# Two blocks of layer 0's modulation: from TensorE in the attention to VectorE, ScalarE and an adding DMA in the projections

## The chip, the cores and the metric

The kernel runs on 1 core of one Trainium2 chip. The metric is device time in microseconds (us), taken as the median of several runs; the kernel before took 1288.5 us (3 runs, 1287.41 to 1289.77). The profile is one further execution, and its times count from the start of its span.

## The reference

One inference step of a small diffusion backbone with two layers, all in float32, on 512 latent tokens and 128 context tokens (640 in all, width 1024). Layer 0 is multi-head latent attention beside chunked spatial gating, layer 1 a pooling mixer; each is followed by a squared-ReLU MLP of width 4096. What matters here is the modulation, which every layer computes from the conditioning vectors and uses around both of its halves:

```python
mod = (jax.nn.silu(cond) @ w_mod[l] + b_mod[l]).reshape(-1, 1, N_MOD * D_MODEL)
sh1, sc1, g1, sh2, sc2, g2 = jnp.split(mod, N_MOD, axis=-1)
h = rms_norm(x, norm1_g[l]) * (1 + sc1) + sh1
x = x + g1 * mix                       # mix: attention and gating, or pooling
h = rms_norm(x, norm2_g[l]) * (1 + sc2) + sh2
x = x + g2 * squared_relu_mlp(h, w_ff1[l], w_ff2[l])
```

There are two conditioning vectors (one for latent, one for context tokens), so `mod` is two rows of 6 x 1024 numbers per layer. The six blocks are counted j = 0 to 5 below: j=2 is g1 and j=3 is sh2. Of layer 0, j=2 is first used in the residual add behind the output projection (`wo`), j=3 in the norm that follows it.

## The kernel before

**Order of the work.** TensorE runs the stages one after the other, and its products stand in the order in which the program writes them, as do the operations of every other engine: the schedule is written out by hand. After the loading and transposing of x and the first two blocks of the modulation (j = 0 and 1) come the products with `w_in`: `kv`, then `qa` (line 966 on), `v` and `u` (`z_block`, line 833), then `q` from `w_qx`, the gating, keys and values, the attention in 40 steps (line 1377 on), the output projection with `w_out`, and the two MLPs. A float32 product is made as three passes over a high and a low part of each operand (`mm3`, lines 828 to 830).

**Weights.** The class `Weights` (line 137) holds one list of items, in the order in which they are to be handled. An item's 512 KB or less are loaded by SP into a raw buffer (line 190); then the item is handled by `pump` (line 196): for a weight, ScalarE rounds it to a high part (line 218) and VectorE subtracts (line 228) into a slot of the weight pool. An item with a `use` of its own, as a block of the modulation, needs no slot. There are 5 raw buffers (`RAWB`); `raw_cap` bounds how many are out at a time, and an item can bring its own cap (`caps`), which then stays. `loads` issues the next loads in list order whenever `used` gives a buffer back in the program's order; on the chip SP's queue waits there until the buffer's last reader is done. `pump(n)` handles up to n items and stops at a full pool or at the held item; `need` handles items until the wanted one is there. Where an item's `use` returns a second half (`rest`), `pump` handles the following item between its two halves, and then skips its next call. In the projections the pool has 4 slots, and `pump(2)` stands behind each of the four qa, v and u items (each item is two k of 128 rows).

**The modulation of layer 0, j = 2 to 5.** `add_mod` puts 16 items into the list, eight for g=1 (j = 2, 3) and eight for g=2 (j = 4, 5). Each loads two raw buffers of 512 KB, and `mod_use` (line 361) multiplies them on TensorE: four products of 32 x 512 columns, one in each quarter of the array (line 367). After the eighth, the sum is copied, transposed by `mod_end` (line 387) and the bias added. The items are held (`st.hold`) until the projections are done and run in the attention's steps, one in each step but two of six.

**The modulation of layer 1.** `vmods` makes it without TensorE. Block j has eight items (k = 0 to 7) of one raw buffer each, and `vmod_use` (line 473) does for each: VectorE multiplies by the first conditioning vector's weight and adds to `acc[0]` (line 482; at k=0 it only multiplies, line 480); ScalarE multiplies the buffer in place by the second one (line 487; at k=0 into `acc[1]`); GpSimd adds it to `acc[1]` (line 489). Both sums lie in raw buffers. `st.later` counts handled items: three after the last block `vmod_sum` adds up the 128 rows on TensorE (line 499), four after it `vmod_end` transposes and adds the bias. These 48 items stand between the weights of layer 0's MLP, from block 1 on, one behind each weight, with a cap of 3 raw buffers. In that MLP `pump` stands behind each pair of products, and each tile of weights serves both parts of the 640 tokens.

**An adding DMA** is used in one place before (line 225): where `lo` is None, at the start of layer 1's MLP, GpSimd's queue adds `w_ff` from memory to the negated high part.

The lines that the change and the steps of the prediction touch are: 196 to 250 (`pump`), 473 to 526 (`vmod_use`, `vmod_sum`, `vmod_end`, `vmods`), 536 to 560 (the list), 833 (`z_block`), 920 (`kv_post`, whose last scaling is line 941), 950 (`ckv_post`: transposes on TensorE, evacuated by lines 956 and 957, run from the steps of `bg` within qa), 966 to 984 (qa), 996 (`qa_post`), 1034 (v's gelu), 1038 (`v_post`).

## Time and profile before

| | us |
|---|---|
| median of 3 runs | 1288.5 (1287.41 to 1289.77) |
| the profiled execution | 1284.05 |
| its span, first to last instruction | 1281.8 |
| TensorE busy in the span | 1253.5 |
| VectorE busy | 815.1 |
| ScalarE busy | 555.1 |
| GpSimd busy | 199.7 |

The rows further down come from a page of the profile and from more detailed answers on the same trace. PE is TensorE's matmul side, PEld its weight loads, DVE VectorE, ACT ScalarE, POOL GpSimd, SP the queue that issues most loads. `L367` is line 367 of the kernel; `out<-in` names tiles, `x128` counts instructions. A row of a timeline begins with the start and the duration in us. In rows of one line or tile the three numbers with slashes are the shortest, median and longest duration in ns, followed by the starts of the first and the last in us. A float32 product by `mod_use` or `vmod_sum` is recorded as two instructions, so four products count x8. Products overlap in TensorE's pipeline, so the busy time of a group is less than count times duration. "DMA to landing" counts from the issue of a DMA to its completion; the shares of DMA queues are shares of the 16 engines' time in the stretch. The granted clock is given as a share of 2.4 GHz.

### The profile page before, as it was taken

To read this page: it belongs to the slowest core of one execution; us is meant where nothing else is said; L and a number is where in the kernel's file an instruction comes from. 1 tells how busy PE (TensorE), PEld (TensorE's weight loads), DVE (VectorE), ACT (ScalarE), POOL (GpSimd) and SP (SyncE) were. 2 spreads that over 40 slices of the span, in tenths; PEclk is the share of its full clock that TensorE was granted. 3 is DMA by queue.
4 is the path that set the end of the run, shared out by engine and by line. 5 is a ranking of instruction groups with operands and counts; after the bars stand their busy time and mean duration, and the time that the engine had idled before them with its cause. 6 is when DMAs were issued, how large, how long until landed. Compare 5 with 4: busy or idle time off the path is not lost.

```text
span 1281.8 us, 20770 instructions
## 1 busy us (share of the span) xinstructions
PE 1253.5 (98%) x8308; PEld 1181.9 (92%) x8308; DVE 815.1 (64%) x1557; ACT 555.1 (43%) x1001; POOL 199.7 (16%) x178
## 2 busy tenths in 40 slices
PE   6999999999999999999999999999999999999997
PEld 5899875689999999999999999879999999999997
DVE  5753864564776565656565637676887666676664
ACT  4445454553453434334343423834235425254253
POOL 0010322221113131313231324310000000000001
PEclk9999999999999999999999999799999999999998
DMA  8742297350335444444444440912213232132212
GB/s 303 261 162 68 81 233 253 123 186 13 118 117 153 127 132 133 147 133 148 132 148 126 154 148 5 235 25 66 66 34 99 64 101 68 64 100 70 95 33 83
DMA packets 65375, 154.08 MB, mean 120 GB/s; under 512 B 5200, under 2 KB 22096, under 8 KB 64768
## 3 DMA queue, kind: packets, MB, share of 16 engines
q1 hardware_dynamic: 61360, 142.53, 34.0%
q0 software_dynamic: 3632, 10.16, 3.8%
q8 instruction: 65, 1.06, 0.3%
q14 instruction: 30, 0.25, 0.1%
q10 hardware_dynamic: 288, 0.08, 0.0%
HBM read 144.21 MB, written 5.39 MB: 117 GB/s over the span
## 4 chain that ended last, share of the span: by engine, by line
PE 84%; DVE 8%; ACT 5%; issue 1%; DMA 1%; POOL 0%; DVEq 0%; ACTq 0%; POOLq 0%
PE dn_ps L829 12%; PE dn_ps L828 12%; PE dn_ps L830 12%; PE up_ps L828 8%; PE up_ps L830 8%; PE up_ps L829 8%; PE o_ps L1329 1%; PE wo_ps L828 1%; PE wo_ps L829 1%; PE wo_ps L830 1%; PE mod_ps L367 1%; PE t_ps L1296 1%; DVE w L586 1%; PE s_ps L828 1%; PE v_ps L828 1%
## 5 line engine op out<-in xcount | busy, mean ns | idle before, releaser
L828 PE MATMUL dn_ps<-aa,w 128*128 128x320 f32 (+4 forms) x1024 | 318.3, 311 | 0.0
L829 PE MATMUL dn_ps<-aa,w 128*128 128x320 f32 (+4 forms) x1024 | 317.7, 310 | 0.0
L830 PE MATMUL dn_ps<-aa,w 128*128 128x320 f32 (+4 forms) x1024 | 317.0, 310 | 0.5 <-DVE w L228 0.5
L828 PE MATMUL up_ps<-h,w 128*128 128x320 f32 (+2 forms) x800 | 249.9, 312 | 1.3 <-ACT h L775 1.3
L829 PE MATMUL up_ps<-h,w 128*128 128x320 f32 (+2 forms) x800 | 248.0, 310 | 1.1 <-DVE h L779 1.1
L830 PE MATMUL up_ps<-h,w 128*128 128x320 f32 (+2 forms) x800 | 248.7, 311 | 0.2 <-DMA w<-w_ff 0.2
L1434 DVE SCALAR_TENSOR_TENSOR x<-dn_ps,mod,x 128x328 f32<-128x328 f32 (+5 forms) x360 | 145.4, 435 | 117.6 <-PE dn_ps L830 116.7
L828 PEld LDWEIGHTS dn_ps<-aa,w 128*128 128x128 f32 x1024 | 193.1, 189 | 1.8 <-issue 0.8
L830 PEld LDWEIGHTS dn_ps<-aa,w 128*128 128x128 f32 x1024 | 193.0, 188 | 0.8 <-DVE w L228 0.8
L829 PEld LDWEIGHTS dn_ps<-aa,w 128*128 128x128 f32 x1024 | 193.0, 188 | 0.1
L228 DVE TENSOR_TENSOR w<-raw,w 128x1024 fp32r<-128x1024 f32 (+4 forms) x122 | 151.9, 1249 | 46.4 <-ACT w L218 45.3
L218 ACT ACTIVATE w<-raw 128x1024 fp32r<-128x1024 f32 (+4 forms) x131 | 132.7, 1026 | 109.7 <-DMA raw<-w_ff 84.9
L828 PEld LDWEIGHTS up_ps<-h,w 128*128 128x128 f32 x800 | 151.2, 189 | 4.9 <-issue 3.4
L829 PEld LDWEIGHTS up_ps<-h,w 128*128 128x128 f32 x800 | 151.4, 189 | 1.6 <-DVE h L779 1.6
L830 PEld LDWEIGHTS up_ps<-h,w 128*128 128x128 f32 x800 | 151.0, 189 | 0.5 <-DMA w<-w_ff 0.5
L489 POOL TENSOR_TENSOR acc<-acc,raw 128x1024 f32<-128x1024 f32 x42 | 100.7, 2398 | 303.6 <-ACT raw L487 299.9
L581 ACT ACTIVATE w<-raw 128x512 fp32r<-128x512 f32 x84 | 51.0, 625 | 108.5 <-DVE raw L588 108.5
L487 ACT ACTIVATE raw<-raw,cs 128x1024 f32<-128x1024 f32 x42 | 48.3, 1149 | 63.3 <-DVE acc L482 58.8
L1963 POOL TENSOR_TENSOR y<-y,fg 128x1024 f32<-128x1024 f32 x1 | 2.4, 2395 | 406.9 <-ACT y L1959 406.9
L1508 DVE TENSOR_TENSOR r<-r,up_ps 128x328 f32<-128x328 f32 (+2 forms) x80 | 37.4, 484 | 40.2 <-ACT r L1507 38.4
L1511 DVE TENSOR_TENSOR aa<-r,aa 128x640 fp32r<-128x640 f32 (+3 forms) x52 | 39.7, 764 | 35.6 <-ACT aa L1510 35.6
L586 DVE TENSOR_TENSOR w<-raw,w 128x512 fp32r<-128x512 f32 x84 | 57.7, 687 | 6.8 <-ACT w L581 5.1
(404 smaller groups left out, 2100.3 us busy)
## 6 DMA issues: line engine op xcount, KB each, us to landing
raw<-w_ff SPq DMA_DIRECT2D x126, 512.0 KB, 3.8
raw<-w_mod SPq DMA_DIRECT2D x80, 512.0 KB, 3.8
raw<-w_m SPq DMA_DIRECT2D x16, 512.0 KB, 6.4
raw<-w_out SPq DMA_DIRECT2D x8, 512.0 KB, 4.6
w<-w_ff POOLq DMA_DIRECT2D x8, 512.0 KB, 9.8
kT<-ckvT POOLq DMA_DIRECT2D x4, 768.0 KB, 10.9
xr<-x SPq DMA_DIRECT2D x5, 512.0 KB, 5.4
xs<-x SPq DMA_DIRECT2D x2, 1280.0 KB, 8.9
```

The costliest lines, as they stand in the source:

```text
L218: self.nc.scalar.activation(out=hi, in_=r, func=AF.Copy)
L228: lambda: eng.tensor_tensor(out=lo, in0=r, in1=hi.bitcast(F32), op=ALU.subtract)
L487: act(out=raw if k else acc[1], in_=raw, func=AF.Copy, scale=w[1])
L489: nc.gpsimd.tensor_tensor(out=acc[1], in0=acc[1], in1=raw, op=ALU.add)
L581: act(out=w[:, 0], in_=src, func=AF.Copy)
L586: vec.tensor_tensor(out=w[:, 1], in0=src, in1=w[:, 0].bitcast(F32), op=ALU.subtract)
L828: mm(ps, lhsT=st_[0], rhs=mv[0], start=first, stop=False, skip_group_check=on)
L829: mm(ps, lhsT=st_[0], rhs=mv[1], start=False, stop=False, skip_group_check=on)
L830: mm(ps, lhsT=st_[1], rhs=mv[0], start=False, stop=last, skip_group_check=on)
L1434: vec.scalar_tensor_tensor(out=xv, in0=ps[:, p0:p0 + c1 - c0], scalar=gate[:, d, m:m + 1], in1=xv, op0=ALU.mult, op1=ALU.add)
L1508: vec.tensor_tensor(out=rv, in0=rv, in1=ps, op=ALU.mult)
L1511: vec.tensor_tensor(out=aa[:, 1, lo:hi], in0=r[:, lo:hi], in1=aa[:, 0, lo:hi].bitcast(F32), op=ALU.subtract)
```

## The change

The list of items is changed: the eight g=1 items leave it, and 16 items of the kind of layer 1 (j=2 and j=3 of layer 0, eight blocks each) are put between the weights of the projections by `add_vm`, two behind each of the qa items, of v's last and of u's first three. They bring the cap of 3. In the list, with V for a block: kv7, qa0, V, V, qa2, V, V, qa4, V, V, qa6, V, V, v0, v2, v4, v6, V, V, u0, V, V, u2, V, V, u4, V, V, u6, wq0 and so on. `pump(4)` stands where `pump(2)` stood behind qa, v and u items; the `pump(2)` behind kv stays. Between the halves of a block `pump` handles the following item only if that is a weight. For layer 0 and layer 1 alike, GpSimd's addition becomes a DMA of its queue that adds the raw buffer to `acc[1]`. The junk output of `v_post`'s squares goes into vn, as the scratch row is now used by `vmod_sum` in that stage.

```diff
@@ -63,6 +63,7 @@
 SPLIT = 3
 SLOW = "ws", "wkv"
 VM_AT = 11, 64
+VM_Z = {("qa", 0): 2, ("qa", 2): 2, ("qa", 4): 2, ("qa", 6): 2, ("v", 6): 2, ("u", 0): 2, ("u", 2): 2, ("u", 4): 2}
 KV_LAG = 1
 KV_AT = {0: 0, 2: 1, 4: 3, 6: 5, 7: 7}
 UK = 192
@@ -239,7 +240,8 @@
 
                 self.skip = False
                 d = self.done
-                self.pump()
+                if self.done < len(self.items) and self.items[self.done][3] is None:
+                    self.pump()
                 rest()
                 self.skip = self.done > d
             n_raw = self.keep.pop(key, len(loads))
@@ -486,7 +488,7 @@
             def rest():
                 act(out=raw if k else acc[1], in_=raw, func=AF.Copy, scale=w[1])
                 if k:
-                    nc.gpsimd.tensor_tensor(out=acc[1], in0=acc[1], in1=raw, op=ALU.add)
+                    nc.gpsimd.dma_start(out=acc[1], in_=raw, accum_op=ALU.add)
 
             return rest
 
@@ -509,7 +511,7 @@
         pt = psa.tile([128, 4, 4, 32], F32, tag="mod", name="vmod_pt")
         for i in range(4):
             nc.tensor.transpose(pt[:, i, :, :].rearrange("p q n -> p (q n)"), row[:, tok(i)], ident)
-        m = const.tile([128, 8, 2], F32, name=f"mod{l}{j}")
+        m = const.tile([128, 8, 2], F32, name=f"vm{l}{j}")
         for h in range(2):
             b = V["b_mod", l][:, 8 * j + 4 * h:8 * j + 4 * h + 4]
             vec.tensor_tensor(
@@ -518,11 +520,11 @@
             )
         mod_done(l, j, m)
 
-    def vmods(l):
-        for j in range(6):
+    def vmods(l, js=range(6)):
+        for j in js:
             for k in range(KD):
                 w = a["w_mod"][l, k * 128:(k + 1) * 128, j * 1024:(j + 1) * 1024]
-                yield ("mod", l, j, k), [(w, (1024,))], 0, vmod_use(l, j, k)
+                yield ("vm", l, j, k), [(w, (1024,))], 0, vmod_use(l, j, k)
             yield None
 
     def tok(t):
@@ -540,20 +542,31 @@
             k0 = KV_AT[f]
             nk = kv_k[k0]
             st.add(("kv", k0), [(rows(w_in, k0, nk, RQ, NKV), (nk, NKV))], nk * NKV)
+    vm = vmods(0, (2, 3))
+
+    def add_vm(key):
+
+        for _ in range(VM_Z.get(key, 0)):
+            v = next(vm) or next(vm)
+            st.items.append(v)
+            st.caps.setdefault(v[0], RAWB - 2)
+
     for k in range(0, KD, 2):
         st.add(("qa", k), [(rows(w_in, k, 2, 0, RQ), (2, RQ))], 2 * RQ)
+        add_vm(("qa", k))
     for k in range(0, KD, 2):
         st.add(("v", k), [(rows(w_in, k, 2, IN - GW, GW), (2, GW))], 1024)
+        add_vm(("v", k))
     for k, n in U_ROWS:
         st.add(("u", k), [(rows(w_in, k, n, RQ + NKV, GW - UK), (n, GW - UK))], n * (GW - UK))
+        add_vm(("u", k))
     for k in range(3):
         st.add(("wq", k), [(a["w_qx"][k * 128:(k + 1) * 128, :], (1024,))], 1024)
     st.add(("ws",), [(a["w_sp"], (1024,))], 1024)
     for k in range(2):
         st.add(("wkv", k), [(a["w_kvx"][k * 128:(k + 1) * 128, :], (1024,))], 1024)
-    add_mod(0, 1)
     add_mod(0, 2)
-    st.hold = ("mod", 0, 1, 0)
+    st.hold = ("mod", 0, 2, 0)
     wo_k = (0, 4, 1, 5, 2, 6, 7, 3)
     for k in wo_k:
         st.add(("wo", k), [(a["w_out"][k * 128:(k + 1) * 128, :], (1024,))], 1024)
@@ -851,7 +864,7 @@
                         bg.step(ZSTEP[nm][k])
             st.free((nm, k0))
             if k0 != items[-1][0]:
-                st.pump(2)
+                st.pump(4)
         return ps
 
 
@@ -980,7 +993,7 @@
                     bg.step()
         st.free(("qa", k0))
         if k0 < KD - 2:
-            st.pump(2)
+            st.pump(4)
     bg.drain()
     ug = [xp.tile([128, NT, GW], F32, tag="X", name=f"ug{i}") for i in range(2)]
     ssq = ug[0].rearrange("p t n -> p (t n)")[:, 0:T]
@@ -1037,8 +1050,7 @@
 
     def v_post():
         for t in range(NT):
-            junk = sc.tile([128, 512], F32, tag="modrow", name="junk5", bufs=1)
-            act(out=junk, in_=ug[1][:, t, :], func=AF.Square, accum_out=ssv[:, t:t + 1])
+            act(out=vn[:, 0, t, :], in_=ug[1][:, t, :], func=AF.Square, accum_out=ssv[:, t:t + 1])
             yield
         rv_ = rsqrt_cols(ssv, NT, GW, "rv")
         yield
```

## Rows read from the trace of the kernel before

**Rows 1.** The page, parts 1 and 4: busy time and the chain, by engine.

```profile
PE 1253.5 (98%) x8308; PEld 1181.9 (92%) x8308; DVE 815.1 (64%) x1557; ACT 555.1 (43%) x1001; POOL 199.7 (16%) x178
...
PE 84%; DVE 8%; ACT 5%; issue 1%; DMA 1%; POOL 0%; DVEq 0%; ACTq 0%; POOLq 0%
```

**Rows 2.** Groups of lines, 130 to 300: busy us, mean ns | idle.

```profile
L367 PE MATMUL mod_ps<-raw,cs 128*32 128x512 f32 x128 | 19.0, 605 | 0.0
...
L387 PE MATMUL mod_pt<-ident,modrow 128*128 128x128 f32 x8 | 1.2, 272 | 0.0
```

**Rows 3.** TensorE's products by tile: ns min/median/max, first/last start.

```profile
L828 PE MATMUL qa_ps<-hh,w x48: 303/310/396, 58.6 to 81.7; 128*128 128x328 f32 x24, 128*128 128x312 f32 x24
...
L828 PE MATMUL v_ps<-w,hh x40: 387/393/478, 82.1 to 111.5; 128*128 128x512 f32 x40
...
L828 PE MATMUL u_ps<-w,hh x40: 302/308/312, 112.2 to 129.2; 128*128 128x320 f32 x40
```

**Rows 4.** Timeline of VectorE, 40 to 130: start and duration in us.

```profile
63.33 2.07 DVE L941 SCALAR_TENSOR_TENSOR kvt<-kvt,rkvy,gkv 128x256 f32<-128x256 f32 x5
...
88.48 2.49 DVE L228 TENSOR_TENSOR w<-raw,w 128x1024 fp32r<-128x1024 f32 x2 [1.07 <-ACT w L218]
```

**Rows 5.** Layer 1's modulation by lines: ns min/median/max, first/last start.

```profile
L480 DVE TENSOR_SCALAR acc<-raw,cs x6: 744/748/749, 362.1 to 685.8; 128x1024 f32<-128x1024 f32 x6
...
L482 DVE SCALAR_TENSOR_TENSOR acc<-raw,cs,acc x42: 1270/1276/1280, 368.3 to 734.1; 128x1024 f32<-128x1024 f32 x42
...
L487 ACT ACTIVATE raw<-raw,cs x42: 1132/1153/1156, 369.7 to 735.4; 128x1024 f32<-128x1024 f32 x42
...
L489 POOL TENSOR_TENSOR acc<-acc,raw x42: 2383/2399/2415, 370.9 to 736.7; 128x1024 f32<-128x1024 f32 x42
```

**Rows 6.** DMA issues, time to landing, and two queues' shares (798 to 840).

```profile
raw<-w_mod SPq DMA_DIRECT2D x80, 512.0 KB, 3.8
...
w<-w_ff POOLq DMA_DIRECT2D x8, 512.0 KB, 9.8
...
DMA to landing us min/median/max: 7.1/9.8/11.5
...
L1135 POOL DMA_DIRECT2D kT<-ckvT x2: 617/630/644, 159.4 to 160.6; - x2
...
DMA to landing us min/median/max: 6.3/9.4/12.4
...
q0 software_dynamic: 2176, 4.19, 56.2%
q1 hardware_dynamic: 2176, 4.19, 32.1%
```

**Rows 7.** Stretches: length, busy (PE, PEld, DVE, ACT, POOL), clock, DMA, GB/s.

```profile
804.00:808.00 4.00, 2.54 (x18) 2.28 (x17) 2.45 (x7) 3.94 (x6) 1.88 (x2) 0.93 1.06 247
808.00:812.00 4.00, 4.00 (x18) 4.00 (x18) 2.05 (x5) 1.24 (x3) 3.00 (x14) 0.50 1.10 250
...
820.00:824.00 4.00, 4.00 (x26) 4.00 (x26) 1.70 (x4) 3.97 (x6) 1.87 (x3) 0.86 0.84 201
```

**Rows 8.** Timelines of ScalarE, GpSimd, SP and TensorE in layer 0's MLP.

```profile
460.38 1.06 ACT L218 ACTIVATE w<-raw 128x1024 fp32r<-128x1024 f32 x1 [3.49 <-DMA raw<-w_ff]
462.04 1.15 ACT L487 ACTIVATE raw<-raw,cs 128x1024 f32<-128x1024 f32 x1 [0.60 <-DVE acc L482]
...
463.34 2.39 POOL L489 TENSOR_TENSOR acc<-acc,raw 128x1024 f32<-128x1024 f32 x1 [3.91 <-ACT raw L487]
...
465.75 0.33 SPq L190 DMA_DIRECT2D raw<-w_mod  x1
...
470.20 2.96 SPq L190 DMA_DIRECT2D raw<-w_ff  x2
...
735.41 1.15 ACT L487 ACTIVATE raw<-raw,cs 128x1024 f32<-128x1024 f32 x1 [2.14 <-DVE acc L482]
...
742.10 1.06 PE L499 MATMUL mod_ps<-acc,cs 128*32 128x512 f32 x8
```

## The prediction

> **What bounds the kernel now.** The page comes first: TensorE is busy 98% of the span and 84% of the chain that ended last is its own [rows 1]. A stage thus loses time only where TensorE is left waiting, and gains only what is taken off TensorE. The groups of lines come next, for what the change takes away: the 16 items of the attention (each 4 products, recorded as 8 instructions) keep TensorE busy for 19.0 us in all, the two sets of transposes behind them for 1.2 us [rows 2]. No idle time stands before the items' products, so they cost their own time there. Third, the tiles of the projections give the places in which the new work is put: qa starts at 58.6, v at 82.1, u at 112.2, and u's last three products start from 129.2 on [rows 3]. Last, DMA and GpSimd rows price the new step, an adding DMA, which the kernel has so far only as 8 DMAs that add w_ff to a tile.
>
> **What goes.** 8 of the 16 items and one of the two sets of transposes leave TensorE in the attention: 19.0/2 + 1.2/2 = 10.1 us. I take all of it: **-10.1 us**. Should the softmax of those steps (VectorE, ScalarE) end last instead, it is 0. The 16 loads of 512 KB are only moved, so SP issues as many as before.
>
> **What comes, and in which order it is queued.** Reading the new order: qa0, V0, V1, qa2, V2, V3, qa4, V4, V5, qa6, V6, V7, v0, v2, and so on (V0 to V7 are the blocks of j=2). Before qa's first products qa0 and V0 are handled; behind them (pump of 4) V1, qa2, V2, V3, qa4, V4; behind the second quarter V5, qa6, V6, V7, v0, v2. Each handled item counts down the lag of 3, so the four products that sum j=2 stand on TensorE directly **behind the second quarter of qa**, and TensorE takes its products in order. They need V7's add. Every add but the first of a j is a DMA that reads and writes the same tile, so each waits on GpSimd for the landing of the one before: 7 links. No row of this kernel shows two such DMAs into one tile. The Trainium skill, DMA: Bandwidth & Descriptors, section Two DMAs through the same engine are not ordered, says that only the completion semaphore orders them, which speaks against this change.
>
> *Start of the chain.* V1's multiply stands on VectorE behind kv's last scaling, which ends at 65.4 [rows 4]. V0 ahead of kv's evacuations moves that by some 0.7 (its multiply, 0.75 [rows 5]). Then VectorE 1.28 and ScalarE 1.15 [rows 5]: 68.5. TensorE's wait for qa2, now handled behind V1's multiply, lies inside the chain.
>
> *One link.* The adding DMAs landed after 7.1 to 11.5 us [rows 6]; the first is the 7.1, and it had plain loads beside it at both ends. The nearest copy from SBUF to SBUF, larger (768 KB) and not adding, took 6.3 at least [rows 6]. A plain load of 512 KB takes 3.8 [rows 6]. By shares an adding DMA holds the engines longer: 56.2% of 42 us for 8 is 2.95 us each, the plain ones 32.1%, so 1.69 [rows 6]. I take 6.5, between 6.3 and 7.1, since here too loads run beside it. From below 3.8: then the buffers bind. There are three raw buffers (cap 3, two of the five hold the sums), V4's load waits until V2's add has landed, and load, multiply, scaling are 3.8 + 1.28 + 1.15 = 6.2, so two links take at least 3.8 + 6.2, one 5.0. From above: 8.5, between 7.1 and the median of 9.8 under full engines.
>
> *j=2.* 68.5 + 7 x 6.5 = 114.0. Only then follow the sum (8 instructions, 1.1 [rows 8]), the other half of qa ((82.1 - 58.6)/2 = 11.7 [rows 3]) and four transposes (0.6 [rows 2]): v starts at 127.4 instead of 82.1.
>
> *j=3.* V8 to V15 come from behind v's first quarter on. VectorE reaches v6's low part 6.4 us after the start of v (88.48 [rows 4]); that part (half of 2.49), 0.75 for V8, 1.28 and 1.15 for V9 [rows 5] put V9's add 10.8 us after it. The sum stands behind u's first quarter: 127.4 + 10.8 + 7 x 6.5 = 183.7. Before, that quarter ended at 112.2 + 17.3/4 = 116.5 [rows 3]. TensorE is **67.2 us** late, and the sum itself is 1.1 more. What is queued behind the waits: on SP qa4, qa6 and v0 behind the release of V1's, V3's and V5's buffers; on VectorE ckvT's low parts behind V4's multiply, hence TensorE's transposes of ckvT; on ScalarE v's gelu behind V15's scaling. These run out beside the chain, not after it.
>
> *Clock.* TensorE idles for tens of microseconds twice. Where it had work for 2.54 of 4 us, the granted clock fell from 0.93 to 0.50, that is 1.2 GHz, and came back only between 820 and 824 [rows 7]: some 13 us, at most 6.5 lost. Here the fall lies in the wait and only the way back costs; I take half, 3 us, twice: **+6**, bounds 0 and 13.
>
> **Layer 1's blocks** lose GpSimd's add of 2.4 us [rows 5], for the same DMA. There SP issues V's load 0.02 us after that add ends (463.34 + 2.39 = 465.73, issue 465.75) and W's load behind it [rows 8]. With a landing L counted from the scaling's end (463.19), V's issue passes W's (470.20) when L exceeds 7.0. Both loads then run one behind the other: two pairs take L, 5.5 for the loads (3.8 and the 1.69 that the other holds the engines) and 2.8 from W's landing to the end of V's scaling (460.38 to 463.19 [rows 8]), at L = 6.5 some 7.4 us a pair. The stretch offers 7.8 on average (6 + 42 blocks from 362.1 to 734.1 [rows 5]), with TensorE never short of weights. So nearly all is covered by the weights made ahead; where bursts are lost I take **+4**, bounds 0 and 25 (L = 8.5: 8.4 a pair, 0.6 x 48 less what is made ahead). The tightest of the six sums there comes 5.5 us behind the last scaling (736.6 and 742.1 [rows 8]), where 6.5 costs 1.
>
> At nothing: the square of v writes into vn instead of a scratch tile (same operation), and the names.
>
> **Sum:** 67.2 + 1.1 + 6 - 10.1 + 4 = +68.2. The profiled execution took 1284.05 us (span 1281.8 and 2.25 around it) and would take 1352.3; the median of the runs shown, 1288.5, is 4.45 above it, and the same sum on it is **1357 us**. Bounds of the link alone (14 links in all): at 5.0 the chains are 21 shorter and layer 1 costs nothing, 1332; at 8.5 they are 28 longer, with 21 more in layer 1, 1406.
>
> By the skill's fit for one such DMA (2.0 us plus bytes at 436 GB/s, same page, section Anatomy of one DMA) 512 KB land after 3.2; a link would be (3.2 + 6.2)/2 = 4.7 and the time 1328, an estimate. The trace disagrees for adding DMAs, with 7.1 as its least.
>
> **Rivals.**
> - *The adds do not hold each other up* (they follow without waiting for the landing). Then the three buffers bind: V keeps one for 6.2 + 6.5 = 12.7, W for 6.1 (3.8, 1.06 for its copy, half of 2.49 [rows 4, 8]); two V and a W are 31.5 over three, 10.5, 5.3 a block in place of 6.5: 17 shorter over 14 blocks, **1340**. For it: nothing in the rows excludes it. It stays slower.
> - *The chain is hidden, faster.* With x the time by which one add holds up the next, for small x only j=2 shows: 7x - 0.2 late, plus 1.1 for the second sum and 3 for the clock. Against 10.1 that breaks even at **x = 0.9 us**; below it TensorE gains up to 10.1 less the sums, **1280**. Against it: 3.8 for a plain load, 2.4 for the add on GpSimd. For it: my order of the queue being wrong, so that the sum stands much further behind and the blocks load earlier than I read.
> - *Layer 1 becomes bound by the adds.* Above L = 7.3 a pair no longer fits 7.8. At 9.8 it is 9.0, 1.2 x 48 = 58 us, with the link of 6.5 kept in the projections: **1411**. For it: loads and adds together need 2 x 1.69 + 2.95 = 6.3 us of the engines per pair of 7.8. Against it: only one add at a time is out, where before's adding DMAs overlapped.
> - *Moved work without the chain's cost:* VectorE and ScalarE merely delay evacuations and eat the 10.1: **1288**. Against it: VectorE has room in most of qa and v.
>
> **How the numbers follow.** Chances: serial chain 0.66, adds not held up 0.06, layer 1 bound 0.10, a smaller loss 0.03, no difference 0.03, hidden 0.12. A measurement of this kernel can tell 0.2%, some 2.6 us, from no change. So faster 0.12, same 0.03, slower 0.85. The range runs from 1315, somewhat below the bound for the shortest link, to 1395, short of the end where both chain and layer 1 are at their worst; what it leaves out is the hidden chain and that corner.
>
> **What would show it.** Right: TensorE idle before the line of the sum in two places, released by an adding DMA, tens of microseconds each; GpSimd's DMA issues spaced by some 6.5; v starting near 127 and j=3's sum near 184; 64 instead of 128 products of the old kind, the attention shorter by 10; the granted clock low after each wait. Wrong: qa still ending near 82, or issues closer than 5 us. Layer 1's term is wrong if TensorE waits there for DMA or for w.

## The result, and the profile after

The changed kernel takes 1442.5 us (median of 4 runs, 1433.8 to 1446.8) against 1288.0 for the kernel before (4 runs): a ratio of 1.119, with a 95% interval from 1.117 to 1.122. I had forecast 1357 us with a range of 1315 to 1395. The direction was right; the size was short by 85 us, outside the range.

The page, parts 1 and 4, of the kernel after (as [rows 1]):

```profile
PE 1279.7 (89%) x8264; PEld 1194.0 (83%) x8264; DVE 822.1 (57%) x1576; ACT 569.9 (40%) x1017; POOL 147.0 (10%) x192
...
PE 32%; DMA 17%; DVE 7%; ACT 7%; issue 3%; POOL 0%; SPq 0%; ACTq 0%; DVEq 0%; POOLq 0%
DMA acc<-raw 11%; PE dn_ps L841 7%; PE dn_ps L843 7%; PE dn_ps L842 7%; DMA raw<-w_ff 7%; PE up_ps L841 3%; PE up_ps L842 3%; PE up_ps L843 3%; ACT raw L489 1%; DVE w L599 1%; ACT w L219 1%; DVE w L229 1%; DVE raw L601 1%; PE mod_ps L501 1%; ACT w L594 1%
```

TensorE's own share of the chain fell from 84% to 32%, and the adding DMA `acc<-raw`, which was not in the kernel, stands first with 11%. The span grew from 1281.8 to 1438.0, by 156.2 us. Where it grew is read from the first product of each stage. The answers by tile, after (as [rows 3], with the scores, the first `up` product of layer 0's MLP and layer 1's pooling added):

```profile
L841 PE MATMUL qa_ps<-hh,w x48: 303/312/643, 61.0 to 137.2; 128*128 128x328 f32 x24, 128*128 128x312 f32 x24
...
L841 PE MATMUL v_ps<-w,hh x40: 387/395/482, 137.7 to 168.1; 128*128 128x512 f32 x40
...
L841 PE MATMUL u_ps<-w,hh x40: 302/310/633, 168.7 to 219.7; 128*128 128x320 f32 x40
...
L841 PE MATMUL s_ps<-kT,qh x72: 273/312/417, 267.1 to 345.3; 128*128 128x320 f32 x64, 128*128 128x128 f32 x8
...
L841 PE MATMUL up_ps<-h,w1h x32: 299/312/397, 413.8 to 442.2; 128*128 128x328 f32 x16, 128*128 128x312 f32 x16
...
L2060 PE MATMUL pool_ps<-dif,wp x64: 432/436/514, 949.8 to 1008.9; 128*128 128x320 f32 x32, 128*128 128x328 f32 x32
```

The same answers of the kernel before, for the three tiles that [rows 3] does not hold:

```profile
L828 PE MATMUL s_ps<-kT,qh x72: 273/311/417, 175.3 to 264.0; 128*128 128x320 f32 x64, 128*128 128x128 f32 x8
...
L828 PE MATMUL up_ps<-h,w1h x32: 299/312/397, 332.3 to 360.7; 128*128 128x328 f32 x16, 128*128 128x312 f32 x16
...
L2048 PE MATMUL pool_ps<-dif,wp x64: 432/435/514, 794.9 to 854.8; 128*128 128x320 f32 x32, 128*128 128x328 f32 x32
```

The scores start 91.8 us later (267.1 against 175.3): that is lost **in the projections**. Between the scores and the `up` products 10.3 us come back (146.7 against 157.0): **the attention's gain**. From the first `up` product to the pooling 536.0 us pass instead of 462.6: 73.4 more **in layer 0's MLP**, which I had put at 4. The rest, 1.3 us, lies behind. Of the 91.8, 2.4 are there before qa starts (61.0 against 58.6). In the runs below that leave everything ahead of qa as in the kernel before, qa starts between 59.1 (run 2) and 61.1 (run 8), so differences of up to some 2.5 us between such starts say nothing; counted from qa's start, the scores come 89.4 us later.

TensorE's waits in the projections (58 to 270; us in total, times, longest), after:

```profile
PE mod_ps L501 <- DMA acc<-raw: 25.7, 2, 15.0
PE mod_ps L501 <- DVE acc L484: 16.9, 2, 12.9
PE ckvT_ps L967 <- DVE ckvT L970: 15.6, 1, 15.6
PE u_ps L841 <- ACT ug L1047: 10.1, 1, 10.1
```

The timeline of GpSimd (start, duration), the adding DMAs of layer 0, after; those of j=2, and the end of j=3:

```profile
71.42 0.90 POOL L491 DMA_DIRECT2D acc<-raw  x1 [1.60 <-ACT raw L489]
79.09 0.85 POOL L491 DMA_DIRECT2D acc<-raw  x1 [6.77 <-DMA acc<-raw]
84.93 0.85 POOL L491 DMA_DIRECT2D acc<-raw  x1 [4.99 <-DMA acc<-raw]
93.41 0.85 POOL L491 DMA_DIRECT2D acc<-raw  x1 [7.63 <-DMA acc<-raw]
...
114.87 0.85 POOL L491 DMA_DIRECT2D acc<-raw  x1 [6.44 <-DMA acc<-raw]
...
178.79 0.86 POOL L491 DMA_DIRECT2D acc<-raw  x1 [4.82 <-DMA acc<-raw]
194.86 0.86 POOL L491 DMA_DIRECT2D acc<-raw  x1 [15.21 <-ACT raw L489]
```

In j=2 GpSimd is released by the landing of the DMA before, as forecast; six spacings from 71.42 to 114.87 make 7.24 us each. Of these 6.71 on average are the landing, which counts from the start of the issue, and 0.53 pass from the landing to the next issue. The spacings alternate, 5.84 from 79.09 and 8.48 from 84.93, with the loads that SP issues beside them (timeline of SP, after):

```profile
78.61 0.38 SPq L191 DMA_DIRECT2D raw<-w_in  x1
84.44 0.80 SPq L191 DMA_DIRECT2D raw<-w_mod  x2
92.93 0.38 SPq L191 DMA_DIRECT2D raw<-w_in  x1
```

An add beside one load landed after 5.3 us (79.09), one beside two after 7.9 (84.93). So it is with all 56 of the kernel: the five with under 3 us of raw buffers' loads beside them landed after 4.5 to 5.3 us, the 24 with over 9 us of loads (two together count twice) after 7.2 to 8.8. The loads in turn wait for the adds: SP waited 86.1 us in 14 waits (58 to 270) for the landing of an add, since the buffer that it adds cannot be loaded again before. The last row of the timeline of GpSimd shows what I had not read: 15.2 us in which GpSimd waited for ScalarE (8.2 of them after the DMA before had landed), because j=3's last two blocks stand behind v's gelu, squares and scalings in ScalarE's and VectorE's queues.

Layer 0's MLP. TensorE's waits from 440 to 940, the largest two, SP's largest, and five adding DMAs in a row of one j, after:

```profile
PE mod_ps L501 <- DMA acc<-raw: 49.0, 6, 10.2
PE dn_ps L841 <- DVE x L1446: 3.5, 2, 2.6
```

```profile
SPq L191 <- DMA acc<-raw: 297.2, 42, 9.9
```

```profile
467.83 0.85 POOL L491 DMA_DIRECT2D acc<-raw  x1 [7.75 <-ACT r L1519]
476.38 0.85 POOL L491 DMA_DIRECT2D acc<-raw  x1 [7.70 <-issue]
489.08 0.85 POOL L491 DMA_DIRECT2D acc<-raw  x1 [11.85 <-ACT raw L489]
496.51 0.86 POOL L491 DMA_DIRECT2D acc<-raw  x1 [6.58 <-ACT raw L489]
505.13 0.86 POOL L491 DMA_DIRECT2D acc<-raw  x1 [7.76 <-ACT raw L489]
```

GpSimd's adds at the same place before; with the 463.34 of [rows 8] they are 7.07 to 7.08 apart:

```profile
470.42 2.39 POOL L489 TENSOR_TENSOR acc<-acc,raw 128x1024 f32<-128x1024 f32 x1 [4.69 <-ACT raw L487]
477.49 2.41 POOL L489 TENSOR_TENSOR acc<-acc,raw 128x1024 f32<-128x1024 f32 x1 [4.69 <-ACT raw L487]
```

Before, a weight and a block came every 7.07 us where nothing stood between them, which is the pace at which TensorE uses weights; over the 36 spacings between the seven adds of each j the mean was 7.0. After, the same 36 have a median of 8.5 and a mean of 8.7. Of the 36, 24 adds are issued 0.5 us behind the landing of the one before. Of the other 12, ten follow ScalarE's scaling by 0.3 us. The one at 489.08 shows why the scaling was late: it comes 12.70 us behind its predecessor, which had landed at 482.54, whereupon SP loaded a weight into the buffer set free (issue 482.60), and ScalarE rounded that weight before it scaled the block. From the first add of one j to the first of the next 77.5 us pass on average in place of 65.0, and six times 12.5 make 75 us, about what was lost. TensorE does not show that as waits for weights but stops once per j, at the sum. The stage, and one stretch around one sum (length; busy of PE, PEld, DVE, ACT, POOL; granted clock, DMA share, GB/s), the stage before, the stage after and the stretch after:

```profile
332.30:794.90 462.60, 462.52 (x3158) 456.04 (x3157) 288.85 (x460) 180.09 (x249) 117.37 (x62) 1.00 0.42 131
```

```profile
413.80:949.80 536.00, 482.40 (x3158) 464.79 (x3158) 276.67 (x460) 177.76 (x249) 52.63 (x62) 0.95 0.59 154
```

```profile
510.00:520.00 10.00, 6.08 (x22) 4.41 (x23) 2.49 (x3) 1.06 (x1) 0.00 (x0) 0.66 0.68 179
```

TensorE was idle for 53.6 of the 536.0 us. It was also busy 19.9 us longer with the same 3158 instructions: the granted clock falls in the wait (0.66 on average in the last row), and the sum's own products, in which a part of the wait hides, take 1061 ns in the median against 617 in run 1 below. So 49.0 us of waiting at the sums go with 73.4 us lost. The DMA engines were busy 0.62 of the time from 440 to 940, so they had room on average; but the landing depends on the traffic beside it, as in j=2 above. No run took the loads away from beside the adds, so how much of a landing is its own and how much that traffic is not shown.

### The profile page after: what moved, and what is told of

It is laid out like the page before. It is cut to its first block, busy times and chain, and to the rows that moved or that the text cites. A ratio compares the mean times of both kernels' runs of the same rounds, so it can differ in the third digit from the quotient of the medians.

```text
span 1438.0 us, 20845 instructions
## 1 busy us (share of the span) xinstructions
PE 1279.7 (89%) x8264; PEld 1194.0 (83%) x8264; DVE 822.1 (57%) x1576; ACT 569.9 (40%) x1017; POOL 147.0 (10%) x192
## 4 chain that ended last, share of the span: by engine, by line
PE 32%; DMA 17%; DVE 7%; ACT 7%; issue 3%; POOL 0%; SPq 0%; ACTq 0%; DVEq 0%; POOLq 0%
DMA acc<-raw 11%; PE dn_ps L841 7%; PE dn_ps L843 7%; PE dn_ps L842 7%; DMA raw<-w_ff 7%; PE up_ps L841 3%; PE up_ps L842 3%; PE up_ps L843 3%; ACT raw L489 1%; DVE w L599 1%; ACT w L219 1%; DVE w L229 1%; DVE raw L601 1%; PE mod_ps L501 1%; ACT w L594 1%
## 5 line engine op out<-in xcount | busy, mean ns | idle before, releaser
L229 DVE TENSOR_TENSOR w<-raw,w 128x1024 fp32r<-128x1024 f32 (+4 forms) x122 | 144.7, 1189 | 102.8 <-ACT w L219 101.7
L841 PEld LDWEIGHTS up_ps<-h,w 128*128 128x128 f32 x800 | 153.3, 192 | 10.3 <-issue 6.7
L842 PEld LDWEIGHTS up_ps<-h,w 128*128 128x128 f32 x800 | 153.4, 192 | 2.4 <-DVE h L792 2.3
L843 PEld LDWEIGHTS up_ps<-h,w 128*128 128x128 f32 x800 | 152.9, 191 | 0.5 <-DMA w<-w_ff 0.5
L484 DVE SCALAR_TENSOR_TENSOR acc<-raw,cs,acc 128x1024 f32<-128x1024 f32 x56 | 71.7, 1281 | 66.5 <-DMA raw<-w_mod 66.4
L501 PE MATMUL mod_ps<-acc,cs 128*32 128x512 f32 x64 | 24.6, 961 | 91.6 <-DMA acc<-raw 74.7
L1446 DVE SCALAR_TENSOR_TENSOR x<-dn_ps,vm,x 128x128 f32<-128x128 f32 (+3 forms) x192 | 78.0, 435 | 48.6 <-PE dn_ps L843 48.5
L491 POOL DMA_DIRECT2D acc<-raw x56 | 48.0, 857 | 528.9 <-ACT raw L489 228.0
L489 ACT ACTIVATE raw<-raw,cs 128x1024 f32<-128x1024 f32 x56 | 64.0, 1142 | 88.1 <-DVE acc L484 84.0
L1446 DVE SCALAR_TENSOR_TENSOR x<-dn_ps,mod,x 128x328 f32<-128x328 f32 (+2 forms) x168 | 63.8, 433 | 36.6 <-PE dn_ps L843 36.5
```

The costliest lines, as they stand in the source:

```text
L229: lambda: eng.tensor_tensor(out=lo, in0=r, in1=hi.bitcast(F32), op=ALU.subtract)
L484: vec.scalar_tensor_tensor(out=acc[0], in0=raw, scalar=w[0], in1=acc[0], op0=ALU.mult, op1=ALU.add)
L489: act(out=raw if k else acc[1], in_=raw, func=AF.Copy, scale=w[1])
L491: nc.gpsimd.dma_start(out=acc[1], in_=raw, accum_op=ALU.add)
L501: mm(ps[32 * q:32 * q + 32, :], lhsT=one, rhs=acc[q % 2][:, 512 * (q // 2):512 * (q // 2) + 512], start=True, stop=True, tile_position=(0, ...
L841: mm(ps, lhsT=st_[0], rhs=mv[0], start=first, stop=False, skip_group_check=on)
```

## The experiments

The theory at the start, A: the adding DMA's latency, in a chain of adds into one tile, costs it all.

**1. GpSimd's add put back in both layers**, everything else as after.

```diff
-                    nc.gpsimd.dma_start(out=acc[1], in_=raw, accum_op=ALU.add)
+                    nc.gpsimd.tensor_tensor(out=acc[1], in0=acc[1], in1=raw, op=ALU.add)
```

> The changed kernel, with GpSimd's own add in place of the adding DMA in both layers (the move, the counts of items handled per step and the rest stay). Theory A, the latency of the chained adding DMAs costs it all: layer 0's MLP gives back its 73 us, the attention keeps its 10, and of the projections' 92 the greater part comes back, since a link is then 2.4 us of GpSimd and not 7.2; what stays there is the 16 loads and the two sums, at 0 to 30. 1280 to 1310 us, likeliest 1295. Rival B, the moved work itself (16 loads more, VectorE and ScalarE passes ahead of their lows, a lower clock) holds up the projections: 60 us or more of the 92 stay, 1340 us or more.

Measured: 1335.6 us, ratio 1.037 (1.034 to 1.040). From the first `up` product to the pooling 462.6 us pass (383.8 to 846.4), exactly as before the change: the MLP's loss was the adding DMA. In the projections theory A fails, and rival B's 60 us stay, though its total of 1340 is missed by 4. The scores start 60.4 us later than before, so only 31.4 of the 91.8 went with the DMA:

```profile
L841 PE MATMUL s_ps<-kT,qh x72: 273/311/417, 235.7 to 315.3; 128*128 128x320 f32 x64, 128*128 128x128 f32 x8
```

The adds of j=2 still follow each other at (97.74 - 70.96)/6 = 4.5 us, though one takes 2.4. GpSimd now waits for ScalarE, which waits for VectorE's multiply, and that for loads; SP in turn waited 61.3 us in 14 waits (58 to 200) for GpSimd's adds to give the buffers back. Two of the adds, run 1:

```profile
89.46 2.34 POOL L491 TENSOR_TENSOR acc<-acc,raw 128x1024 f32<-128x1024 f32 x1 [3.12 <-ACT raw L489]
...
97.74 2.34 POOL L491 TENSOR_TENSOR acc<-acc,raw 128x1024 f32<-128x1024 f32 x1 [1.14 <-ACT raw L489]
```

**2. The kernel before, with the adding DMA in layer 1** (its only blocks of this kind).

```diff
-                    nc.gpsimd.tensor_tensor(out=acc[1], in0=acc[1], in1=raw, op=ALU.add)
+                    nc.gpsimd.dma_start(out=acc[1], in_=raw, accum_op=ALU.add)
```

> The kernel before, with the adding DMA in place of GpSimd's add in layer 1 alone (its only vector blocks); nothing is moved. Theory A: the six sums in layer 0's MLP each wait for the last add of a chain at 8.5 us a link where TensorE takes 7.07 us a weight: 6 x 12.2 = 73 us, 1361 us, and TensorE waits 6 times at the sum's matmuls. Rival B, the 73 us come from the new order of handling or from what the move leaves behind: 1288 to 1295 us and no such wait.

Measured: 1370.5 us, ratio 1.065 (1.060 to 1.069); the MLP takes 543.2 us (335.0 to 878.2), 80.6 more than before, and TensorE waits six times at the sums, 52.7 us in all. Theory A holds here: this one line, with nothing moved, costs about half of the whole loss. Why it is 7 more than in the changed kernel stays open.

**3. The adding DMA in layer 0 alone.**

```diff
-                    nc.gpsimd.dma_start(out=acc[1], in_=raw, accum_op=ALU.add)
+                    if l == 0:
+                        nc.gpsimd.dma_start(out=acc[1], in_=raw, accum_op=ALU.add)
+                    else:
+                        nc.gpsimd.tensor_tensor(out=acc[1], in0=acc[1], in1=raw, op=ALU.add)
```

> The changed kernel with the adding DMA in layer 0's two blocks alone, GpSimd's add in layer 1. Theory A: the projections' 92 us and the attention's -10 stay, layer 0's MLP takes what it took before: 1288 + 81 = 1369 us, and this run's excess and that of the run with layer 1 alone sum to the 154 of the whole change. Rival B (as above): 1430 us or more.

Measured: 1365.0 us, ratio 1.060 (1.056 to 1.065). The scores start at 267.6 as in the changed kernel, and the MLP takes 462.6 as before. The excesses of runs 2 and 3, 82 and 77, sum to 159, about the 154 of the whole: the two places hardly depend on each other.

**4. One more weight between one j of layer 1 and the next, its sums one item later.** The 48 items start three weights earlier.

```diff
-VM_AT = 11, 64
+VM_AT = 8, 72
...
-VM_LAG = 3, 4
+VM_LAG = (3, 4), (4, 5)
...
+            yield None
             yield None
```

> The changed kernel with one more weight without a block between two of layer 1's blocks, and its sum one item later; the work is the same, the adding DMAs as many. Theory A, TensorE waits in order at the sum for a chain that is late: a chain has one more weight (7.07 us) to end in, so each of the six waits of 9 us at the sum shrinks to 2 or less, and the time falls by some 6 x 8 = 48 us, to about 1395. Rival C, the adds hold raw buffers so long that the weights themselves come late, at 8.5 us a pair: the waits go to the weights' matmuls, and the time falls by under 15 us, to 1427 or more.

Measured: 1430.6 us, 12 less than the changed kernel (in the MLP 7.6 less, 528.4 us); that is rival C's figure. Its waits are there in part. TensorE's two largest and SP's largest from 440 to 940, run 4:

```profile
PE mod_ps L501 <- DMA acc<-raw: 18.5, 3, 6.6
PE dn_ps L842 <- ACT w L219: 18.3, 4, 5.4
```

```profile
SPq L191 <- DMA acc<-raw: 300.7, 42, 10.8
```

The wait at the sum fell from 49.0 to 18.5, but 18.3 appear where there was none: at weights that ScalarE could not round in time, and ScalarE waited for their loads. The loads waited for raw buffers that the adds held, as SP's row says, once for each of the 42 adds. From the first add of one j to the first of the next 77.5 us pass, as in the changed kernel, although each j now has one more weight: the pace is that of adds and loads, and the placement of the sum decides only where the late pairs show.

**5. Accumulators out of the raw buffers** (with GpSimd's add). Layer 0's two sums lie in one weight slot; all five raw buffers take loads.

```diff
-                mod_ps[l, j] = [rawp.tile([128, 1024], F32, tag="raw", name=f"acc{c}") for c in range(2)]
+                if l == 0:
+                    st.of["vm", j], w = st.slots.take([128, 2, 1024], F32R)
+                    mod_ps[l, j] = [w[:, c, :].bitcast(F32) for c in range(2)]
+                    st.tiles["vm", j] = w
...
-            st.caps.setdefault(v[0], RAWB - 2)
```

> The changed kernel with GpSimd's add, and layer 0's accumulators in one of the 4 weight slots in place of two of the 5 raw buffers, so that up to u all 5 take loads (they took 3). Theory D: of the 60 us that the projections still lose with GpSimd's add, the greater part is the loads that run only 3 deep while each buffer is held through a multiply on VectorE, one on ScalarE and an add on GpSimd; then 25 us or more come back, 1310 us or less. Rival E, the order in which TensorE must take the sums, the blocks' transposes and ckvT behind VectorE's multiplies: the loads come earlier and the time stays within 8 us of 1336. Rival F, three weight slots are fewer than the weights need: slower than 1336.

Measured: 1312.5 us, ratio 1.020 (1.017 to 1.023); the scores start at 214.3, 21.4 us earlier than in run 1. Theory D comes nearest, 2 us short of its figure: about that much of the projections' loss was loads that ran three deep, net of the weight slot that the sums now take.

**6. Three raw buffers alone, in the kernel before.**

```diff
     st.hold = ("mod", 0, 1, 0)
+    st.caps["qa", 0] = RAWB - 2
```

> The kernel before with at most 3 raw buffers in loads from qa's first weight to the attention, no block moved. Theory D in its strong form (3 buffers are too few for the projections' own weights): 1300 us or more. In its weak form (too few only with a block beside each weight): within 4 us of 1288.

Measured: 1288.5 us, ratio 0.9998 (0.9986 to 1.0010). The weak form: three buffers are enough for the weights, too few with a block's load beside each.

**7. The blocks spread** over qa (1 behind each weight), v (2) and u (1), with run 1's add.

```diff
-VM_Z = {("qa", 0): 2, ("qa", 2): 2, ("qa", 4): 2, ("qa", 6): 2, ("v", 6): 2, ("u", 0): 2, ("u", 2): 2, ("u", 4): 2}
+VM_Z = {("qa", 0): 1, ("qa", 2): 1, ("qa", 4): 1, ("qa", 6): 1, ("v", 0): 2, ("v", 2): 2, ("v", 4): 2, ("v", 6): 2, ("u", 0): 1, ("u", 2): 1, ("u", 4): 1, ("u", 6): 1}
```

> The changed kernel with GpSimd's add, and the 16 blocks spread: one behind each weight of qa, two behind each of v, one behind each of u (it was 2, 2, 2, 2 in qa, 2 at v's last weight, 2, 2, 2 in u). Theory D: qa's weights wait for half as many loads, and v's stage (30 us, in which the transfers were busy a fifth of the time before) hides its eight; 20 to 45 us of the 47 come back: 1291 to 1316 us, likeliest 1300. Rival E (TensorE waits at two sums and at ckvT wherever the blocks stand): 1325 us or more.

Measured: 1335.1 us, no different from run 1: rival E. TensorE's two largest waits from 58 to 200, run 7:

```profile
PE Rq_ps L702 <- DVE rqy L688: 12.1, 1, 12.1
PE ckvT_ps L967 <- DVE ckvT L970: 12.0, 1, 12.0
```

Neither is a block's own result. VectorE takes its instructions in order; a block's multiply that waits for its load, or takes up to 3.4 us in place of 1.28 beside GpSimd's adds (see run 9), holds up `ckvT`'s low part or the query's scale behind it, and TensorE waits for those.

**8. Every second add by DMA**, in the kernel before.

```diff
-                    nc.gpsimd.tensor_tensor(out=acc[1], in0=acc[1], in1=raw, op=ALU.add)
+                    if k % 2:
+                        nc.gpsimd.dma_start(out=acc[1], in_=raw, accum_op=ALU.add)
+                    else:
+                        nc.gpsimd.tensor_tensor(out=acc[1], in0=acc[1], in1=raw, op=ALU.add)
```

> The kernel before, where every second add (odd k) of layer 1's blocks is an adding DMA, the others GpSimd's. Theory A (a block's chain of adds is late only when its links together exceed the weights' demand, 7.07 us a weight): two links take 8 + 2.4 us where two weights take 14.1, so nothing is lost: 1288 to 1294 us. Rival G (each adding DMA costs its share, through its traffic or the buffer it holds): half of the 82 us, 1322 to 1335.

Measured: 1300.9 us, ratio 1.011 (1.005 to 1.016): 12.7 us lost, 13.1 in the MLP, where half of run 2's loss would be 41 (of each j's seven adds four are DMAs). Neither figure is met, but the loss does not go with the number of adding DMAs: it is mostly a threshold, as theory A says. What is left is at the sums, behind whose last block (k=7) an adding DMA still stands. TensorE's largest wait from 330 to 830, run 8:

```profile
PE mod_ps L502 <- DMA acc<-raw: 6.3, 6, 2.3
```

**9. VectorE makes both accumulators in layer 0**, on top of run 5.

```diff
             def rest():
+                if l == 0:
+                    if k:
+                        vec.scalar_tensor_tensor(
+                            out=acc[1], in0=raw, scalar=w[1], in1=acc[1], op0=ALU.mult, op1=ALU.add
+                        )
+                    else:
+                        vec.tensor_scalar(out=acc[1], in0=raw, scalar1=w[1], scalar2=None, op0=ALU.mult)
+                    return
```

> The run with the accumulators in a weight slot, and in layer 0 VectorE makes both accumulators (two multiply-adds of 1.28 us a block), ScalarE and GpSimd none. In that run VectorE's multiply of 1.28 us took up to 3.4 and a weight's low of 0.95 up to 3.2 while GpSimd's adds ran beside it. Theory H, the two engines keep each other from running: without GpSimd's adds VectorE's rows are back at 1.28 and 0.95, and although VectorE has 16 passes more, the time falls by 8 us or more, to 1304 or less. Rival E, the order of TensorE's and VectorE's queues alone: within 6 us of 1312. Rival I, VectorE is now the bound of qa: slower than 1318.

Measured: 1303.8 us, ratio 1.013 (1.010 to 1.016), theory H's figure at its edge; the scores start at 204.7, 9.6 us earlier, though VectorE has more to do. The timeline of VectorE and of GpSimd in run 5:

```profile
68.27 0.95 DVE L229 TENSOR_TENSOR w<-raw,w 128x768 fp32r<-128x768 f32 x1
69.14 4.62 DVE L489 SCALAR_TENSOR_TENSOR w<-raw,cs,w 128x1024 f32<-128x1024 f32 x2
73.69 3.16 DVE L229 TENSOR_TENSOR w<-raw,w 128x768 fp32r<-128x768 f32 x1
76.77 3.35 DVE L489 SCALAR_TENSOR_TENSOR w<-raw,cs,w 128x1024 f32<-128x1024 f32 x1
```

```profile
69.62 9.42 POOL L496 TENSOR_TENSOR w<-w,raw 128x1024 f32<-128x1024 f32 x3 [1.40 <-ACT raw L494]
81.50 2.37 POOL L496 TENSOR_TENSOR w<-w,raw 128x1024 f32<-128x1024 f32 x1 [2.46 <-ACT raw L494]
```

The same operation on the same shape takes 0.95 us at 68.27 and 3.16 at 73.69, when GpSimd adds; and three adds of GpSimd take 9.42, while one alone takes 2.37. In run 9 all 14 multiply-adds of line 489 are back at 1275 to 1279 ns. That the two engines hold each other up is shown by these rows; the 9.6 us are the net of that, of ScalarE's and GpSimd's passes that are gone, and of VectorE's 16 more, and no run takes these apart.

**10. Run 9 with the blocks spread** as in run 7.

```diff
-VM_Z = {("qa", 0): 2, ("qa", 2): 2, ("qa", 4): 2, ("qa", 6): 2, ("v", 6): 2, ("u", 0): 2, ("u", 2): 2, ("u", 4): 2}
+VM_Z = {("qa", 0): 1, ("qa", 2): 1, ("qa", 4): 1, ("qa", 6): 1, ("v", 0): 2, ("v", 2): 2, ("v", 4): 2, ("v", 6): 2, ("u", 0): 1, ("u", 2): 1, ("u", 4): 1, ("u", 6): 1}
```

> The same with VectorE making both accumulators, the 16 blocks spread 1 behind each weight of qa, 2 of v, 1 of u. Theory D and H together: no stage has more than 15 us of added VectorE work in its time, and the projections lose 10 to 25 us: 1290 to 1303 us. Rival E, TensorE waits for VectorE's queue (ckvT, the query's scale) behind a multiply whose load is late, wherever the blocks stand: 1305 or more.

Measured: 1304.9 us, no gain, between the two theories' figures. Handled four items at a time, the blocks bunch anyway: from 72.50 to 84.94 VectorE runs eight multiply-adds and three low parts without a pause, and TensorE waits 6.7 us for the `ckvT` behind them.

**11. The blocks in the attention**, behind TensorE's modulation, with GpSimd's add and run 5's slots; `VM_Z` is empty and qa, v and u are handled in steps of 2.

```diff
     add_mod(0, 2)
     st.hold = ("mod", 0, 2, 0)
+    st.items += [v for v in vm if v]
...
+        if i == WO_AT - 2:
+            st.flush(2)
         if i == WO_AT:
+            st.flush()
             st.hold = None
```

> The 16 blocks stay in the attention, behind the modulation that TensorE still makes there, with GpSimd's add and the accumulators in the attention's weight slots; the projections handle their weights in steps of 2 as before the change. Theory J, what costs is only where the blocks were put: the projections take what they took before (s_ps starts at 175 +-3), the attention is shorter by the 19 us of TensorE's matmuls less 9 that were hidden, as in the changed kernel: 1275 to 1282 us. Rival I, VectorE and GpSimd, beside the softmax, become the attention's bound (VectorE 47 us of its 89 before, 21 more now): the attention takes 85 us or more, 1284 or more.

Measured: 1315.6 us, ratio 1.023 (1.020 to 1.025): rival I. The projections are free again (scores at 177.7), but from the scores to `wo` 126.3 us pass (177.7 to 304.0) in place of 98.5. TensorE's and GpSimd's waits from 170 to 310, run 11:

```profile
POOL P L1284 <- DVE m L1281: 45.0, 14, 17.8
...
PE t_ps L1315 <- POOL P L1284: 15.4, 9, 2.7
```

The softmax's scaling on GpSimd (`P`) now stands behind adds and waits for a VectorE that is behind multiplies, and the transposes on TensorE wait for it.

**12. j=2 in v and u, j=3 in the attention**, VectorE making both accumulators (with run 11's lines in the attention and run 14's steps).

```diff
+VM_Z = {("v", 0): 2, ("v", 2): 2, ("v", 4): 1, ("v", 6): 1, ("u", 0): 1, ("u", 2): 1}
...
+    st.items += [v for v in vm if v]
```

> VectorE makes both accumulators; block j=2 in v and u (2, 2, 1, 1 and 1, 1 behind their weights), block j=3 in the attention behind TensorE's modulation, none in qa; qa and u are handled in steps of 2 as before the change. Theory K, VectorE's passes cost what they put in front of work that TensorE waits for, and v and the attention have idle VectorE time for 10 to 20 us each: the projections lose 3 to 10 us, the attention gains 3 to 8: 1284 to 1294 us. Rival I, the attention, whose VectorE had 47 us of work in 89, becomes bound by it: 1295 us or more.

Measured: 1301.4 us, ratio 1.012 (1.005 to 1.019), the best of the moved versions, though not clear of runs 9 and 10, and still 14 slower than before. Theory K's gain in the attention did not come; the time is in rival I's range, but no row shows VectorE as the attention's bound. The scores start 13.7 us late (189.0), and from there to `wo` 102.7 us pass, 4 more than before: the eight blocks in the attention took back more than TensorE's absent products gave.

**13. Loads alone**: run 9 without 24 of layer 0's 32 multiply passes, all loads kept.

```diff
-            else:
+            elif l or k == 1:
                 vec.scalar_tensor_tensor(out=acc[0], in0=raw, scalar=w[0], in1=acc[0], op0=ALU.mult, op1=ALU.add)
```

(and the same for `acc[1]`).

> The run in which VectorE makes both accumulators, with the multiplies of k = 2 to 7 of layer 0's two blocks left out (24 of 32 passes, 31 us of VectorE), all loads kept. Theory K, the rest of the projections' loss is VectorE's passes: 1292 us or less. Rival L, it is the 16 loads ahead of the weights' own: within 5 us of 1304.

Measured: 1292.0 us, ratio 1.005 (1.003 to 1.006). The scores start at 193.1: VectorE's 24 passes were 11.6 us of what was left, as theory K says (without them the raw buffers also come free sooner, which is in the 11.6), but 17.8 us remain that loads, sums and the new order make up between them. Of these 2.7 stand ahead of qa's start (61.3 against 58.6), where starts scatter.

**14. Smaller steps**: run 10 with qa and u handled 2 items at a time.

```diff
             if k0 != items[-1][0]:
-                st.pump(4)
+                st.pump(4 if nm == "v" else 2)
...
         if k0 < KD - 2:
-            st.pump(4)
+            st.pump(2)
```

> The spread run with VectorE making both accumulators, but qa and u handled in steps of 2 items, v in steps of 4 (all were in steps of 4). Theory K: fewer passes stand in a row ahead of ckvT's low and the weights' lows, whose row of eight between 72 and 85 us held TensorE for 6.7 us; 1290 to 1300 us. Rival: the passes come later but as many, within 3 us of 1305.

Measured: 1325.1 us, 20 slower than run 10, against both. The wait for `ckvT` is gone, and in its place TensorE waits for the weights themselves. Its largest wait, 58 to 310, run 14:

```profile
PE v_ps L856 <- DVE w L229: 11.8, 4, 4.5
```

The step of 4 thus brings the weights in time, at the price of blocks that stand in rows.

## Why the prediction was wrong

**Layer 1's blocks** were the step that failed: "nearly all is covered by the weights made ahead; ... I take **+4**, bounds 0 and 25". The changed kernel and run 2 put it at 73 to 81, and my own sign against it, TensorE waiting there for a DMA, is the first row of that stage. Three things were wrong in it. "The stretch offers 7.8 on average" took the mean over the whole MLP, with the slots that hold no block in it; inside a j the need is 7.0 to 7.07, and the rows for it lay next to one that I had taken, the 463.34 of [rows 8]. The landing, 6.5 in my sum, was 7.5 in the median there, and my pair of 7.4 us came out at 8.7 in the mean. And nothing covered the difference: 1.7 us too long, 36 times, make 61 between the adds, and from the last add of one j to the first of the next 25.3 us pass instead of 22.9, so the next j did not catch up either. Either size alone would have cost less, by my own formula: (7.4 - 7.0) x 48 = 19 us, or (8.7 - 7.8) x 48 = 43. The rival that named this (1411) asked for the right quantity; I gave it 0.10.

**The projections** came out at +91.8 where my terms make 67.2 + 1.1 + 6 = 74.3. The chain, its releaser and the in-order wait at the sum are all there. In j=2 the first add was issued at 71.42 (forecast 68.5), and seven links ended at 122.98 (114.0), 7.37 each where I took 6.5; the landing alone was near my figure in the mean, and I had left out the 0.53 behind it. v started at 137.7 (127.4). In j=3 the first add came 13.6 us after that (10.8), and its seven links took 55.3 us until 206.51 (45.5), the 15.2 us gap among them, from a place in ScalarE's and VectorE's order that I had read too early. In the other direction, j=3's sum stands behind u's second quarter and not its first, as I had read the queue: 20 of the 40 products of each pass ran before it. That makes TensorE 4.3 us less late. With 73.4 in place of 4 and 91.8 in place of 74.3 my sum gives 1444.

But the reason that I gave for the projections was only half right, and that only the runs showed. Taking the chain away gives back 31.4 us, not 68. Of the 91.8, in the order in which the runs took them off: the adding DMA 31.4 (run 1), three instead of five raw buffers for loads 21.4 (run 5), the adds on GpSimd and the scalings on ScalarE against 16 more passes of VectorE 9.6 (run 9), 24 VectorE passes 11.6 (run 13), and 17.8 not taken apart, 2.7 of them ahead of qa. Another order would share them out otherwise, since each hides behind the one before. My lower bound of a link, 5.0 "then the buffers bind", was the true second limit (4.5 measured in j=2 of run 1), and the time I gave with it, 1332, is within 4 us of run 1. Some of that is luck: by that bound the scores come 53 us late, and they came 60.4 late. The rival "moved work without the chain's cost", 1288, was wrong by 47: VectorE does have room on average, but not at the moment at which TensorE needs it.

**The attention** is the step that held: -10.1 forecast, -10.3 measured.

```profile
L369 PE MATMUL mod_ps<-raw,cs 128*32 128x512 f32 x64 | 8.6, 604 | 0.0
```

These are the 64 products that stay (as [rows 2], 200 to 360): 19.0 became 8.6.

**The clock.** The granted clock was 0.50 from 85 to 122, 0.69 from 123 to 130 and 1.00 from 130 to 137: the fall lies in the wait and only the way back costs, as I had taken it. From j=2's last landing to v 14.7 us pass where my terms without the clock make 13.4, so that way back cost some 1.3 where I took 3. No run separates the term of 6 as a whole. In layer 0's MLP I had put the clock at nothing, and it is part of the 19.9 us that TensorE was busy longer there.

**The fit that I cited against my own link** (the Trainium skill, DMA: Bandwidth & Descriptors, section Anatomy of one DMA: 3.2 us for 512 KB) is far off for this form: of 56 adding DMAs the landing was 4.5 at least and 7.4 in the median. The same page's section Two DMAs through the same engine are not ordered says that the ordering an author has is the completion semaphore. The trace agrees as far as it can: every add of j=2 was issued 0.53 us behind the landing of the one before.

No version tried beats the kernel before (1287 to 1288). The gain is bounded by 10 us, and run 13 shows that the loads, the sums and a quarter of the passes in the projections already cost 17.8 (15.1 from qa's start).

## What to carry to other kernels

Price a step of a chain by the landing under the traffic that it will have beside it, plus the time to the next issue, and hold it against the interval at which its consumer comes back in that very loop, not against an average of the stretch: 1.7 us too much per step cost 73 us here, while run 8, with 24 of the 42 adds as DMAs, lost 13. An engine with idle time on average is not free: what is put into its queue stands in front of what TensorE waits for, and buffers lent to the new work are missing for the old. When a limit is removed, ask what stands directly behind it; my own lower bound named it.

## What the runs showed that I had not expected

VectorE and GpSimd run almost one after the other when both work on two operands from SBUF: 0.95 became 3.16 us and three adds of 2.37 took 9.42 (run 5). From 69.14 on, VectorE's four operations and GpSimd's three adds would take 4.8 and 7.1 us alone, and together they took 11.0. `ckvT`'s low part, of whose two operands one is TensorE's product `ckvT_ps`, took 0.54 to 0.56 there, also beside an add (83.84). Behind these rows stands a rule that I had not used: the Trainium skill, SBUF — State Buffer, section SBUF: two separate sides, says that the two engines share a pair of ports under an exclusive lock, held for a whole instruction, when VectorE has two inputs in SBUF and GpSimd reads SBUF. The trace agrees, with the 3.16 and the 9.42 above. It is also a price that the adding DMA avoids (VectorE's multiply-adds took 1283 ns in the mean in the changed kernel's projections), but in layer 0's MLP that price was already hidden (462.6 us with GpSimd's add).

The adding DMAs of 512 KB from SBUF to SBUF landed after 4.5 to 8.7 us in layer 0's MLP, with engines that were busy 0.62 of the time, while plain loads of the same size beside them took 4.2 to 4.7 in the median. The issue itself held GpSimd for 0.86 us each.
